# Three 128-token turns of a decoder trunk's token mixers, moved from TensorE to VectorE and DRAM

## The chip, the core and the metric

One core of a Trainium2 chip runs the whole program once. The metric is the device time of that run in microseconds (us), the median of several runs. A core has five engines with queues of their own: TensorE (PE in the profile; its weight loads are PEld), VectorE (DVE), ScalarE (ACT), GpSimd (POOL) and SyncE (SP). Each takes its instructions strictly in the order in which they were written into its queue, so an instruction that waits holds up everything behind it on that engine. Transfers (DMA) are issued here by SyncE, for the weights, and by GpSimd, for everything that bounces through DRAM.

## What is computed

A decoder trunk of two layers over 256 tokens of width 1024. In each layer, between two feed-forward halves, three token mixers work on the same normalised stream:

```python
h = layer_norm(ALPHA * x + 0.5 * swiglu(x, ...), ...)
(dn_q, dn_k, dn_v, dn_b, dn_a, dn_z, sw_q, sw_k, sw_v, xa_q, gates) = split(h @ w_in)
o_dn = deltanet_branch(...)            # gated delta rule, normalised rows times silu(z)
o_sw = sliding_window_attention(...)   # 128-key window, 8 heads, softmax with sinks
o_xa = memory_cross_attention(...)
merged = sum(sigmoid(gates) * einsum('bsnc,ncd->bsnd', [o_dn, o_sw, o_xa], w_branch))
h = layer_norm(ALPHA * h + merged @ w_out, ...)
return layer_norm(ALPHA * h + 0.5 * swiglu(h, ...), ...)
```

Two of these need a turn, a change of which axis lies on the 128 partitions: the softmax weights of the sliding mixer have queries on partitions and are wanted with keys there, and the output rows of the delta mixer have tokens on partitions and are wanted with channels there. The 256 tokens are two blocks of 128; "first" means the first block.

## The kernel before

All matrix products are made in split precision: an operand is a pair hi and lo, and each product is three matmuls, hi by hi, hi by lo and lo by hi (`mm3`, L139). Weights come as one stream of units of 128 x 1024 numbers, 512 KB each (`unit`, L104). For each unit SyncE issues the load into a `raw` tile (L115), ScalarE casts it to `whi` and VectorE subtracts to `wlo` (both in `split`, L125). There are four `raw` tiles and five of each of the others. A load is issued when a `raw` tile comes free, which is when VectorE has made the `wlo` of an older unit. `split` also makes the hi and lo parts of activations, so most of ScalarE's and VectorE's work has line L125.

Inside `mixers` the order of TensorE's instructions is pinned to the order of the code (`pe`, L129). The mixers come in the order cross attention (X), sliding window (S), delta (T). `gates(n)` (L1102) multiplies the stream by the gate weights in eight units and ends each half with two tanh; `branch(n, o)` (L1120) multiplies a mixer's output `o` by four units, in four quarters: first block left and right half, second block left and right half. `weave(work, steps)` (L145) runs the steps listed under n after the n-th unit or quarter of that work, and so fixes the places of the small matmuls. `tc.issue_after(i)` puts what follows behind i on i's engine; `held(f)` does so for all the instructions kept in `late`.

The steps that matter here, each once per layer:

- `w_scores(tb, hh)` (L832): scores and softmax weights of block tb for half hh of the heads; `w_turn(hh)` (L861) turns those of the first block by four PE transposes into PSUM (L137) and a ScalarE copy (L867); `w_leave` and `w_back` (L871, L882) turn those of the second block: VectorE transposes blocks of 32 x 32 (L875), four DMAs on GpSimd's queue write them to DRAM (L878), and DMAs read them back with the blocks in place (L888). `w_values(tb)` (L890) multiplies by the values.
- `leave_v` (L635) sends the delta mixer's values the same way (L640, L644, L648).
- `inverses` (L910) and `double` (L1030): GpSimd inverts 16 x 16 triangles by a chain of 30 small operations (L940, L941) on numbers that it reads back from DRAM (L928); TensorE doubles the inverses in seven steps, with small ScalarE and VectorE operations between them (the copy L995 after the third).
- `rec_o0` (L1094) makes the first block's delta output; `finish` (L1052) normalises it on VectorE and multiplies by silu(z) (L1060, L1061); `finish_turn(c)` (L1063) turns it by four PE transposes and splits it into `oT`, the operand of `branch(2)`.

The turns of block 0 are the steps `w_turn(0)`, `w_turn(1)` in `branch(0)` and `finish_turn(0)` in `gates(2)`.

Of the kernel before, what the change touches and what calls it, by code (L numbers as in the profile page):

```python
# [38 lines left out]
def tile_trunk(ctx, tc, x, xT, mem, memT_, wst, lnp, memln, cvw, rows, cst, out):  # L39
    nc = tc.nc  # L40
# [21 lines left out]
    def T(pool, shape, tag, dt=F32, bufs=None):  # L62
        pool = pn if pool is pu and tag in NEAR else pool
        kw = {} if bufs is None else {"bufs": bufs}
        return pool.tile(shape, dt, tag=tag, name=nm(tag), **kw)
# [4 lines left out]
    def at():  # L70
        return T(psT, [P, 512], "at")
# [64 lines left out]
    def transpose(*a):  # L136
        return pe(nc.tensor.transpose(*a))  # L137
# [422 lines left out]
    def mixers(l, hT, mkT, mv_, post0, post):  # L560
# [74 lines left out]
        def leave_v():  # L635
            turned_v = []
            for tb in range(2):
                z = T(p2, [P, 512], "t2", bufs=4)
                with tc.issue_after(wpr["end"]):
                    wpr["z"] = nc.vector.transpose(z, squares(vT, tb)).ins  # L640
                d = T(pd, [4, 32, 4, P], "tv")
                for a in range(4):
                    with tc.issue_after(late["inverses"]):
                        out_ = nc.gpsimd.dma_start(d[:, :, a].rearrange("t j x -> j t x"), z[32 * a:32 * a + 32].rearrange("j (t x) -> j t x", t=4)).ins  # L644
                turned_v.append(d)
            for tb in range(2):
                with tc.issue_after(out_):
                    late["pool"] = nc.gpsimd.dma_start(vin[:, tb].rearrange("p a h i -> p (a h i)"), turned_v[tb].rearrange("t j a x -> (t j) (a x)")).ins  # L648

        def land_v():  # L650
            for tb in range(2):
# [206 lines left out]
            wpr["end"] = nc.vector.reciprocal(sums, sums).ins  # L858
            late["act"] = [nc.scalar.mul(pr[:, h, :nk], pr[:, h, :nk], sums[:, h:h + 1]) for h in range(4)][-1].ins  # L859

        def w_turn(hh):  # L861
            if hh == 0:
                wpT[0] = T(p2, [P, 2, 4, P], "pt")
            ps = at().rearrange("p (h k) -> p h k", h=4)
            for h in range(4):
                transpose(ps[:, h, :], wpr[0, hh][:, h, :P], ident)
            nc.scalar.copy(wpT[0][:, :, 2 * hh:2 * hh + 2, :].rearrange("p v i q -> p i v q"), ps.rearrange("p (i v) q -> p i v q", v=2))  # L867

        left = []

# [19 lines left out]
        def w_values(tb):  # L890
            if not oS:
                oS.extend(T(pu, [P, 4, S], tag, F32R) for tag in ("u6", "u7"))
            ts = slice(tb * P, (tb + 1) * P)
            pso = at()
            for kb in range(tb + 1):
                for kv in range(2):
                    hs = slice(kv * 64, kv * 64 + 64)
                    if tb:
                        o, w = pso[hs].rearrange("p (y i x) -> p y i x", y=8, i=2), wpT[1][kb].rearrange("p h (a i v x) -> p (h a) i v x", a=4, i=2, v=2)[:, :, :, kv]
                    else:  # L900
                        o, w = pso[hs], wpT[0][:, kv].rearrange("p h q -> p (h q)")
                    matmul(o, swv[:, kb, hs], w, start=kb == 0, stop=kb == tb)
            if tb:
                for y in range(2):
                    late["act"], late["dve"] = split(*(t[:, 2 * y:2 * y + 2, ts].rearrange("p i (a x) -> p i a x", a=4) for t in oS), pso[:, y * S:y * S + S].rearrange("p (a i x) -> p i a x", a=4, i=2))
            else:
                late["act"], late["dve"] = split(oS[0][:, :, ts], oS[1][:, :, ts], pso.rearrange("p (h k) -> p h k", h=4))


        def inverses():  # L910

            cp = T(p2, [P, 16, 2, 4], "t2", bufs=4)
            for c in range(2):
                tmp = T(p2, [P, 4, P], "t2", bufs=4)
                nc.vector.tensor_tensor(tmp, AK[c][:, :, 0, :], over4(cs[:, C_NB:C_NB + P]), op=ALU.mult)
                nc.vector.tensor_reduce(cp[:, :, c], tmp.rearrange("p h (d i) -> p i h d", i=16), axis=AX.X, op=ALU.add)
            dr, dr2 = T(pd, [P, 16 * 8], "dr"), T(pd, [P, 8 * 8], "dr2")
            rows_ = cp.rearrange("p i c h -> p (i c h)")
            for d, r in ((dr, rows_), (dr2, rows_[:, 64:])):
                with tc.issue_after(late["pool"]):  # L920
                    late["pool"] = nc.gpsimd.dma_start(d, r).ins
            x_back()
            tm = [t.rearrange("p a h c -> p (a h c)") for t in TM]
            parts = [tm[0][:, 0:512], tm[0][:, 512:1024], tm[1][:, 0:512]]
            for t, (dst, d) in enumerate(zip(parts, (dr, dr, dr2))):
                src = d.rearrange("(d j) n -> d (j n)", j=16)[:, t % 2 * 512 + t // 2 * 512:][:, 0:512].unsqueeze(1).to_broadcast([8, 16, 512])
                with tc.issue_after(late["pool"]):
                    late["pool"] = nc.gpsimd.dma_start(dst, src).ins  # L928
            masks(1)

            y16 = T(p2, [P, 16, 8], "t2", bufs=4)
            pr16 = T(p2, [P, 15, 8], "t2", bufs=4)
            i16 = cs[:, C_I16:C_I16 + 16].unsqueeze(2).to_broadcast([P, 16, 8])
            with tc.issue_after(late["pool"]):
                nc.gpsimd.tensor_copy(y16, i16)
            for j in range(15):
                n = 15 - j
                row = (parts[j // 4][:, j % 4 * 128:j % 4 * 128 + 128] if j < 8 else parts[2][:, (j - 8) * 64:(j - 8) * 64 + 64]).rearrange("p (i n) -> p i n", n=8)
                row = row[:, j + 1 - j // 8 * 8:]
                nc.gpsimd.tensor_tensor(pr16[:, 0:n], row, y16[:, j:j + 1].to_broadcast([P, n, 8]), op=ALU.mult)  # L940
                nc.gpsimd.tensor_tensor(y16[:, j + 1:16], y16[:, j + 1:16], pr16[:, 0:n], op=ALU.add)  # L941
            late["inverses"] = nc.gpsimd.tensor_tensor(Y32.rearrange("p c h (d i) -> p (c h) d i", d=2), y16.rearrange("p i n -> p n i").unsqueeze(2).to_broadcast([P, 8, 2, 16]),
                                    cs[:, C_BD:C_BD + 32].rearrange("p (d i) -> p d i", d=2).unsqueeze(1).to_broadcast([P, 8, 2, 16]), op=ALU.mult).ins
# [108 lines left out]
        def finish(c, o, sq):  # L1052
            ms = T(p2, [P, 4], "oms")
            nc.scalar.activation(sq, o, AF.Square)
            nc.vector.tensor_reduce(ms, sq, axis=AX.X, op=ALU.add)
            nc.vector.scalar_tensor_tensor(ms, ms, 1.0 / P, qeps[:, c, :], op0=ALU.mult, op1=ALU.add)
            fr = T(p2, [P, 4], "ofr")
            rsqrt(fr, ms, T(p2, [P, 4], "oft"))
            on = fin[c] = T(p2, [P, 4, P], "t2", bufs=4)
            nc.vector.tensor_tensor(on, o, hb(fr), op=ALU.mult)  # L1060
            nc.vector.tensor_tensor(on, on, zs[:, c, :].rearrange("p (h e) -> p h e", h=4), op=ALU.mult)  # L1061

        def finish_turn(c):  # L1063
            if not oT:
                oT.extend(T(pu, [P, 4, S], tag, F32R) for tag in ("u8", "u9"))
            ps = sm().rearrange("p (h c) -> p h c", h=4)
            for h in range(4):
                transpose(ps[:, h, :], fin[c][:, h, :], ident)
            split(oT[0][:, :, c * P:(c + 1) * P], oT[1][:, :, c * P:(c + 1) * P], ps)
# [48 lines left out]
                yield  # L1118

        def branch(n, o):  # L1120
            us = [unit(behind=late["pairs"] if n == 1 and i > 1 else None) for i in range(4)]
            if not mg:
                mg.extend(T(pu, [P, D], f"u{4 + tb}") for tb in range(2))
            gt = gts[n]
# [21 lines left out]
            7: [lambda: w_scores(0, 0)],  # L1146
            8: [lambda: w_scores(0, 1)]})
        weave(branch(0, oX), {
            2: [lambda: w_turn(0)],
            3: [lambda: w_turn(1), leave_v, begin_inverse],  # L1150
            4: [lambda: w_scores(1, 0)]})
        weave(gates(1), {
            1: [double, lambda: w_values(0)],
            2: [lambda: w_scores(1, 1)],
            3: [double, lambda: held(lambda: w_leave(0))],
            5: [double, lambda: held(lambda: w_leave(1)), w_back],
            6: [double],
            7: [double, lambda: held(land_v)],
            8: [double, lambda: held(leave_q)]})
        weave(branch(1, oS), {  # L1160
# [2 lines left out]
            3: [rec_s1, lambda: held(land_q)],  # L1163
            4: [rec_r1]})
        weave(gates(2), {
            1: [rec_o0],
            2: [rec_qs, rec_v1],
            3: [rec_o1],
            5: [lambda: finish_turn(0)],
            8: [lambda: finish_turn(1)]})  # L1170

        def merge_turn(tb, q):
# [168 lines left out]
```

## Time and profile before

| | us |
|---|---|
| median of 3 runs (range) | 1261.83 (1261.32 to 1262.03) |
| the profiled execution, its own time | 1261.66 |
| its span, first to last instruction | 1259.9 |
| TensorE busy in the span | 1248.6 |
| VectorE, ScalarE, GpSimd busy | 880.0, 657.9, 257.0 |
| the mixers' weave, layer 1: `branch(0)` begins, `branch(2)` begins | 321.94, 410.80 |

The granted TensorE clock was 0.998. The span is 1.8 us shorter than the execution's time; what lies around it does not depend on the order inside. Times of rows are us from the span's start; the second layer runs the same code 623.4 us later (its first sliding turn stands at 950.87, that of layer 1 at 327.55). A timeline row gives start, duration, engine, line, operation, tiles written and read, shapes, and in brackets the idle time before it and what ended it. Rows of one line that follow each other may be merged; then x4 or the like stands behind, and one TensorE product in full float32 may stand as two.

### The profile page before, as it was taken

To read this page: it belongs to the slowest core of one execution; us is meant where nothing else is said; L and a number is where in the kernel's file an instruction comes from. 1 tells how busy PE (TensorE), PEld (TensorE's weight loads), DVE (VectorE), ACT (ScalarE), POOL (GpSimd) and SP (SyncE) were. 2 spreads that over 40 slices of the span, in tenths; PEclk is the share of its full clock that TensorE was granted. 3 is DMA by queue.
4 is the path that set the end of the run, shared out by engine and by line. 5 is a ranking of instruction groups with operands and counts; after the bars stand their busy time and mean duration, and the time that the engine had idled before them with its cause. 6 is when DMAs were issued, how large, how long until landed. Compare 5 with 4: busy or idle time off the path is not lost.

```text
span 1259.9 us, 18730 instructions
## 1 busy us (share of the span) xinstructions
PE 1248.6 (99%) x6836; PEld 1062.9 (84%) x6836; DVE 880.0 (70%) x1300; ACT 657.9 (52%) x978; POOL 257.0 (20%) x459
## 2 busy tenths in 40 slices
PE   9999999999999999999999999999999999999997
PEld 6888889999878888888888888899988788888886
DVE  5788567886768776665776665779777588666565
ACT  6556444655665544454454544356657654445441
POOL 1232102003541102221012220020055401122100
PEclk9999999999999999999999999999999999999999
DMA  8988767756565748887668886676565565588871
GB/s 288 318 276 272 262 217 215 225 182 181 182 185 156 247 140 254 245 239 223 219 206 240 261 259 206 214 236 211 161 192 173 163 213 205 187 247 242 243 228 73
DMA packets 82156, 273.60 MB, mean 217 GB/s; under 512 B 13424, under 2 KB 14864, under 8 KB 82064
## 3 DMA queue, kind: packets, MB, share of 16 engines
q1 hardware_dynamic: 66320, 232.40, 57.7%
q0 software_dynamic: 15600, 39.87, 11.0%
q8 instruction: 54, 0.88, 0.3%
q14 instruction: 38, 0.31, 0.1%
q10 hardware_dynamic: 144, 0.13, 0.0%
HBM read 252.20 MB, written 20.15 MB: 216 GB/s over the span
## 4 chain that ended last, share of the span: by engine, by line
PE 97%; ACT 1%; DMA 1%; DVE 0%; issue 0%; SPq 0%; DVEq 0%; ACTq 0%
PE acc L134 87%; PE at L134 4%; PE sm L134 3%; PE sm L137 1%; PE acc L332 1%; PE acc L333 1%; PE acc L335 1%; DMA raw<-in_wst_dram 1%; ACT pp L856 0%; PE at L137 0%; ACT pp L859 0%; ACT whi L125 0%; DVE h L291 0%; DVE h L296 0%; ACT w L995 0%
## 5 line engine op out<-in xcount | busy, mean ns | idle before, releaser
L125 DVE TENSOR_TENSOR wlo<-raw,whi 128x1024 fp32r<-128x1024 f32 (+2 forms) x405 | 485.7, 1208 | 254.6 <-ACT whi L125 252.5
L125 ACT CAST whi<-raw 128x1024 fp32r<-128x1024 f32 (+2 forms) x405 | 413.3, 1029 | 390.0 <-PE acc L134 293.2
L134 PE MATMUL acc<-whi,hT 128*128 128x512 f32 (+1 forms) x1824 | 562.6, 386 | 0.5 <-ACT whi L125 0.5
L134 PEld LDWEIGHTS acc<-whi,hT 128*128 128x128 f32 x1824 | 340.5, 188 | 69.8 <-ACT whi L125 2.2
L134 PE MATMUL acc<-wlo,hT 128*128 128x512 f32 (+1 forms) x912 | 350.9, 385 | 0.0
L134 PE MATMUL acc<-whi,u 128*128 128x512 f32 x812 | 260.3, 393 | 0.0
L134 PEld LDWEIGHTS acc<-wlo,hT 128*128 128x128 f32 x912 | 171.6, 188 | 32.9 <-DVE wlo L125 0.7
L134 PEld LDWEIGHTS acc<-whi,u 128*128 128x128 f32 x812 | 152.3, 188 | 33.7 <-issue 1.6
L362 POOL DMA_DIRECT2D tr<-t x176 | 95.9, 552 | 311.4 <-DVE t L356 309.3
L134 PE MATMUL acc<-wlo,u 128*128 128x512 f32 x406 | 158.3, 390 | 0.0
L134 PE MATMUL acc<-hT,whi 128*128 128x256 f32 x672 | 121.8, 284 | 0.0
L134 PEld LDWEIGHTS acc<-hT,whi 128*128 128x128 f32 x672 | 104.8, 192 | 0.0
L134 PE MATMUL acc<-hT,wlo 128*128 128x256 f32 x336 | 95.2, 283 | 0.0
L134 PEld LDWEIGHTS acc<-wlo,u 128*128 128x128 f32 x406 | 76.3, 188 | 15.3
L363 POOL DMA_DIRECT2D pt<-tr x44 | 24.6, 558 | 195.9 <-DMA tr<-t 134.0
L134 PEld LDWEIGHTS acc<-hT,wlo 128*128 128x128 f32 x336 | 64.4, 192 | 0.0
L353 ACT ACTIVATE t<-acc 128x256 f32<-128x256 f32 x88 | 33.4, 380 | 37.8 <-PE acc L134 37.7
L134 PE MATMUL acc<-u,u 128*128 128x512 f32 x186 | 46.4, 394 | 0.0
L354 DVE TENSOR_TENSOR t<-t,acc 128x256 f32<-128x256 f32 x88 | 36.7, 417 | 8.1 <-ACT t L353 4.1
L134 PEld LDWEIGHTS acc<-u,u 128*128 128x128 f32 x186 | 34.7, 188 | 7.5
L125 DVE TENSOR_TENSOR u<-pt,u 128x512 fp32r<-128x512 f32 x44 | 28.9, 657 | 14.1 <-ACT u L125 14.1
L1138 POOL TENSOR_TENSOR u<-u,gt 128x512 f32<-128x512 f32 x16 | 20.7, 1294 | 88.3 <-DVE gt L1135 88.3
(257 smaller groups left out, 1201.1 us busy)
## 6 DMA issues: line engine op xcount, KB each, us to landing
raw<-in_wst_dram SPq DMA_DIRECT2D x409, 512.0 KB, 4.5
tr<-t POOLq DMA_DIRECT2D x176, 64.0 KB, 4.0
pt<-tr POOLq DMA_DIRECT2D x44, 256.0 KB, 5.3
raw<-in_wst_dram SPq DMA_DIRECT2D x16, 324.0 KB, 5.1
gB<-in_lnp_dram SPq DMA_DIRECT2D x6, 512.0 KB, 5.5
bB<-in_lnp_dram SPq DMA_DIRECT2D x6, 512.0 KB, 6.3
tn<-pp POOLq DMA_DIRECT2D x16, 128.0 KB, 4.0
pt<-tn POOLq DMA_DIRECT2D x8, 256.0 KB, 6.0
```

Source lines behind the costliest of these rows:

```text
L125: return nc.scalar.copy(hi, src).ins, nc.vector.tensor_tensor(lo, src, hi.bitcast(F32), op=ALU.subtract).ins
L134: return pe(nc.tensor.matmul(*a, **k))
L137: return pe(nc.tensor.transpose(*a))
L332: nc.tensor.matmul(ps, hT[0][:, k, ts], hi[:, c], start=k == 0, stop=False)
L333: nc.tensor.matmul(ps, hT[0][:, k, ts], lo[:, c], start=False, stop=False)
L335: nc.tensor.matmul(ps, hT[1][:, k, ts], hi[:, c], start=False, stop=k == KD - 1)
L353: act = nc.scalar.activation(t[:, :, tb, :], g, AF.Silu).ins
L354: ins = nc.vector.tensor_tensor(t[:, :, tb, :], t[:, :, tb, :], u, op=ALU.mult).ins
L362: nc.gpsimd.dma_start(d[:, :, q].rearrange("b c x -> c b x"), z[32 * q:32 * q + 32].rearrange("c (b x) -> c b x", b=4))
L363: back = nc.gpsimd.dma_start(y, d.rearrange("b c q x -> (b c) (q x)")).ins
L1138: nc.gpsimd.tensor_tensor(mg[tb][:, js], mg[tb][:, js], gt[tb][:, js], op=ALU.add)
```

## The change

Three PE turns per layer go, and their work takes the path of `w_leave`:

- `w_turn` becomes `w_leave0` (a VectorE transpose of 128 x 512 per half), `w_out0` (four DMAs of 128 KB to DRAM, behind those of `leave_v`) and `w_back0` (two DMAs back, behind the reads of `leave_v`). `w_values(0)` reads the weights in the layout of the second block and moves from the first to the sixth unit of `gates(1)`. Its result is split in two pieces.
- `finish_turn(0)` becomes `finish_leave` behind `rec_o0` (a VectorE transpose of 128 x 512, four DMAs of 64 KB out, one of 256 KB back) and `finish_land` behind the seventh unit of `gates(2)`: the split from the tile that was read back, put behind the newest weight split on ScalarE and VectorE. The third and fourth weight units of `branch(2)` are split behind it (`behind=`). `finish_turn(1)` stays.
- `w_scores(1, 0)` comes before the last quarter of `branch(0)`, not behind it; `w_scores(1, 1)`, `w_leave(0)` and `w_leave(1)` with `w_back` come a unit sooner in `gates(1)`.
- In `inverses`, the second and third read of the numbers (`w<-dr`) are issued behind `masks(1)`, not ahead of it.

On TensorE, at the end of the second quarter of `branch(0)` in layer 1, this stood before (`acc` is a PSUM accumulator of the branch, `u_554` and `u_555` are hi and lo of X's output, `pp_3225` the sliding weights of half 0, `cs` holds the identity):

```order
L134 MATMUL acc_3339<-wlo_3319,u_554_3165 128x512
L134 MATMUL acc_3339<-whi_3318,u_555_3166 128x512
L137 MATMUL at_3354<-cs,pp_3225 128x128 x4
L134 MATMUL acc_3360<-whi_3300,u_554_3165 128x512
L134 MATMUL acc_3360<-wlo_3301,u_554_3165 128x512
```

and at the end of the third quarter this stands now, where the second turn stood (`swk` are the keys, `u_466` and `bB` hi and lo of the queries of block 1):

```order
L134 MATMUL acc_3355<-whi_3318,u_555_3166 128x512
L134 MATMUL at_3396<-swk_99,u_466_2584 128x512
L134 MATMUL at_3396<-swk_100,u_466_2584 128x512
L134 MATMUL at_3396<-swk_99,bB_2585 128x512
L134 MATMUL at_3401<-swk_99,u_466_2584 128x512
L134 MATMUL at_3401<-swk_100,u_466_2584 128x512
L134 MATMUL at_3401<-swk_99,bB_2585 128x512
L134 MATMUL acc_3424<-whi_3300,u_554_3165 128x512
```

The four transposes of each `w_turn` are gone from the queue, and the six products of `w_scores(1, 0)` stand one quarter earlier.

On ScalarE, around the end of `gates(2)` in layer 1, this stood before (`whi_4199`, `whi_4205` and `whi_4211` are units two, three and four of `branch(2)`; `u_731` is the hi part of `oT`; `sm_4122` and `sm_4185` are the turned first and second block in PSUM; `u_761` and `u_765` are units of the output projection; `gt<-acc` is a gate's tanh):

```order
L125 CAST whi_4199<-raw_4198 128x1024
L125 CAST u_731_4120<-sm_4122 128x4x128
L125 CAST whi_4205<-raw_4204 128x1024
L125 CAST whi_4211<-raw_4210 128x1024
L125 CAST u_761_4238<-raw_4237 128x1024
L1117 ACTIVATE gt_3954<-acc_4100 128x512
L125 CAST whi_4232<-raw_4231 128x1024
L125 CAST u_765_4259<-raw_4258 128x1024
L1117 ACTIVATE gt_3955<-acc_4101 128x512
L125 CAST u_731_4120<-sm_4185 128x4x128
```

and this stands now (`u_740` is the hi part of `oT`, `pt_4011` the tile read back from DRAM, `whi_4209` and `whi_4215` units three and four, `u_767` the output unit that was `u_765`):

```order
L125 CAST whi_4203<-raw_4202 128x1024
L125 CAST u_740_4165<-pt_4011 128x4x4x32
L125 CAST whi_4209<-raw_4208 128x1024
L125 CAST whi_4215<-raw_4214 128x1024
L125 CAST u_763_4242<-raw_4241 128x1024
L1143 ACTIVATE gt_3954<-acc_4109 128x512
L125 CAST whi_4236<-raw_4235 128x1024
L125 CAST u_767_4263<-raw_4262 128x1024
L1143 ACTIVATE gt_3955<-acc_4110 128x512
L125 CAST u_740_4165<-sm_4189 128x4x128
```

The queue is the same but for the second row, which waited for TensorE's turn and now waits for a DMA read.

On GpSimd, behind the reads of `leave_v` (`u_392<-tv`), the first block's weights go out (`tw_3384<-gt_3353`) and back (`pt_3391`), before the second block's (`tw_3546`, `tw_3630`, back into `pt_3635` and `pt_3636`):

```order
L878 DMA tw_3384<-gt_3353 32x8x128 x4
L651 DMA u_392_2081<-tv_3372 128x512
L651 DMA u_392_2081<-tv_3379 128x512
L885 DMA pt_3391<-tw_3384 128x512 x2
L896 DMA tw_3546<-u_626_3543 32x8x128 x4
L1026 COPY w_469_2587<-w_468_2586 32x4x32 x8
L896 DMA tw_3630<-bB_3627 32x8x128 x4
L906 DMA pt_3635<-tw_3546 128x512
L906 DMA pt_3636<-tw_3546 128x512
```

Six DMAs have come in between the delta values and the second block's weights.

The diff, cut to its core:

```diff
@@ leave_v
+            first["behind"] = out_
+            w_out0()
+            out_ = first["out"]
             for tb in range(2):
                 with tc.issue_after(out_):
                     late["pool"] = nc.gpsimd.dma_start(vin[:, tb]..., turned_v[tb]...).ins
+            w_back0()
...
-        def w_turn(hh):
-            if hh == 0:
-                wpT[0] = T(p2, [P, 2, 4, P], "pt")
-            ps = at().rearrange("p (h k) -> p h k", h=4)
-            for h in range(4):
-                transpose(ps[:, h, :], wpr[0, hh][:, h, :P], ident)
-            nc.scalar.copy(wpT[0][:, :, 2 * hh:2 * hh + 2, :]..., ps...)
+        def w_leave0(hh):
+            if not hh:
+                first["z"] = T(p2, [P, 1024], "gt")
+            nc.vector.transpose(first["z"][:, hh * 512:(hh + 1) * 512], wpr[0, hh][:, :, :P].rearrange("p h (m x) -> p m h x", m=4))
+
+        def w_out0():
+            first["d"] = T(pd, [8, 32, 4, P], "tw")
+            for a in range(4):
+                with tc.issue_after(first["behind"]):
+                    first["out"] = nc.gpsimd.dma_start(first["d"][:, :, a]..., first["z"][32 * a:32 * a + 32]...).ins
+
+        def w_back0():
+            wpT[0] = [T(p2, [P, 2, 512], "pt")]
+            for hh in range(2):
+                with tc.issue_after(late["pool"]):
+                    late["pool"] = nc.gpsimd.dma_start(wpT[0][0][:, hh], first["d"][4 * hh:4 * hh + 4]...).ins
...
@@ w_values
-            if tb:
-                for y in range(2):
-                    late["act"], late["dve"] = split(...)
-            else:
-                late["act"], late["dve"] = split(oS[0][:, :, ts], oS[1][:, :, ts], ...)
+            for y in range(2):
+                split(*(t[:, 2 * y:2 * y + 2, ts].rearrange("p i (a x) -> p i a x", a=4) for t in oS), pso[:, y * S:y * S + S]...)
...
@@ inverses
-            masks(1)
+                if not t:
+                    masks(1)
...
+        def finish_leave():
+            z = T(p2, [P, 4, P], "t2", bufs=4)
+            nc.vector.transpose(z, fin[0].rearrange("p h (m x) -> p m h x", m=4))
+            d = T(pd, [4, 32, 4, P], "tf")
+            for q in range(4):
+                nc.gpsimd.dma_start(d[:, :, q].rearrange("m r c -> r m c"), z[32 * q:32 * q + 32])
+            fin["back"] = T(p2, [P, 4, 4, 32], "pt")
+            nc.gpsimd.dma_start(fin["back"].rearrange("p q h x -> p (q h x)"), d.rearrange("m r q c -> (m r) (q c)"))
+
+        def finish_land():
+            oT.extend(T(pu, [P, 4, S], tag, F32R) for tag in ("u8", "u9"))
+            with tc.issue_after(newest[0]), tc.issue_after(newest[1]), tc.issue_after(fin["on"]):
+                fin["landed"] = split(*(t[:, :, 0:P].rearrange("p h (q x) -> p q h x", q=4) for t in oT), fin["back"])
...
         def branch(n, o):
-            us = [unit(behind=late["pairs"] if n == 1 and i > 1 else None) for i in range(4)]
+            us = [unit(behind={1: late.get("pairs"), 2: fin.get("landed")}.get(n) if i > 1 else None) for i in range(4)]
...
         weave(branch(0, oX), {
-            2: [lambda: w_turn(0)],
-            3: [lambda: w_turn(1), leave_v, begin_inverse],
-            4: [lambda: w_scores(1, 0)]})
+            2: [lambda: w_leave0(0)],
+            3: [lambda: w_leave0(1), leave_v, begin_inverse, lambda: w_scores(1, 0)]})
         weave(gates(1), {
-            1: [double, lambda: w_values(0)],
-            2: [lambda: w_scores(1, 1)],
-            3: [double, lambda: held(lambda: w_leave(0))],
-            5: [double, lambda: held(lambda: w_leave(1)), w_back],
-            6: [double],
+            1: [double, lambda: w_scores(1, 1)],
+            2: [lambda: held(lambda: w_leave(0))],
+            3: [double],
+            4: [lambda: held(lambda: w_leave(1)), w_back],
+            5: [double],
+            6: [double, lambda: w_values(0)],
...
         weave(gates(2), {
-            1: [rec_o0],
+            1: [rec_o0, finish_leave],
             2: [rec_qs, rec_v1],
             3: [rec_o1],
-            5: [lambda: finish_turn(0)],
+            7: [finish_land],
             8: [lambda: finish_turn(1)]})
```

More of the change, by code (lines that the diff above doesn't have):

```diff
@@ L859, in w_scores @@
             late["act"] = [nc.scalar.mul(pr[:, h, :nk], pr[:, h, :nk], sums[:, h:h + 1]) for h in range(4)][-1].ins
-        def w_turn(hh):
-            if hh == 0:
-                wpT[0] = T(p2, [P, 2, 4, P], "pt")
-            ps = at().rearrange("p (h k) -> p h k", h=4)
-            for h in range(4):
-                transpose(ps[:, h, :], wpr[0, hh][:, h, :P], ident)
-            nc.scalar.copy(wpT[0][:, :, 2 * hh:2 * hh + 2, :].rearrange("p v i q -> p i v q"), ps.rearrange("p (i v) q -> p i v q", v=2))
+        first = {}
+        def w_leave0(hh):
[6 more added lines that the diff above has]
+                with tc.issue_after(first["behind"]):
+                    first["out"] = nc.gpsimd.dma_start(first["d"][:, :, a].rearrange("m x c -> x m c"), first["z"][32 * a:32 * a + 32].rearrange("x (m c) -> x m c", m=8)).ins
+        def w_back0():
+            wpT[0] = [T(p2, [P, 2, 512], "pt")]
+            for hh in range(2):
+                with tc.issue_after(late["pool"]):
+                    late["pool"] = nc.gpsimd.dma_start(wpT[0][0][:, hh], first["d"][4 * hh:4 * hh + 4].rearrange("m x a c -> (m x) (a c)")).ins
         left = []
@@ L897, in w_values @@
                     hs = slice(kv * 64, kv * 64 + 64)
-                    if tb:
-                        o, w = pso[hs].rearrange("p (y i x) -> p y i x", y=8, i=2), wpT[1][kb].rearrange("p h (a i v x) -> p (h a) i v x", a=4, i=2, v=2)[:, :, :, kv]
-                    else:
-                        o, w = pso[hs], wpT[0][:, kv].rearrange("p h q -> p (h q)")
+                    o, w = pso[hs].rearrange("p (y i x) -> p y i x", y=8, i=2), wpT[tb][kb].rearrange("p h (a i v x) -> p (h a) i v x", a=4, i=2, v=2)[:, :, :, kv]
                     matmul(o, swv[:, kb, hs], w, start=kb == 0, stop=kb == tb)
-            if tb:
-                for y in range(2):
-                    late["act"], late["dve"] = split(*(t[:, 2 * y:2 * y + 2, ts].rearrange("p i (a x) -> p i a x", a=4) for t in oS), pso[:, y * S:y * S + S].rearrange("p (a i x) -> p i a x", a=4, i=2))
-            else:
-                late["act"], late["dve"] = split(oS[0][:, :, ts], oS[1][:, :, ts], pso.rearrange("p (h k) -> p h k", h=4))
+            for y in range(2):
+                split(*(t[:, 2 * y:2 * y + 2, ts].rearrange("p i (a x) -> p i a x", a=4) for t in oS), pso[:, y * S:y * S + S].rearrange("p (a i x) -> p i a x", a=4, i=2))
         def inverses():
@@ L1060, in finish @@
             nc.vector.tensor_tensor(on, o, hb(fr), op=ALU.mult)
-            nc.vector.tensor_tensor(on, on, zs[:, c, :].rearrange("p (h e) -> p h e", h=4), op=ALU.mult)
+            fin["on"] = nc.vector.tensor_tensor(on, on, zs[:, c, :].rearrange("p (h e) -> p h e", h=4), op=ALU.mult).ins
+        def finish_leave():
[10 more added lines that the diff above has]
+                fin["landed"] = split(*(t[:, :, 0:P].rearrange("p h (q x) -> p q h x", q=4) for t in oT), fin["back"])
         def finish_turn(c):
-            if not oT:
-                oT.extend(T(pu, [P, 4, S], tag, F32R) for tag in ("u8", "u9"))
             ps = sm().rearrange("p (h c) -> p h c", h=4)
```

## The prediction

> **What bounds the kernel now.** I read the page first: which engine is busy, and the chain that ended last.
>
> ```profile
> PE 1248.6 (99%) x6836; PEld 1062.9 (84%) x6836; DVE 880.0 (70%) x1300; ACT 657.9 (52%) x978; POOL 257.0 (20%) x459
> PE 97%; ACT 1%; DMA 1%; DVE 0%; issue 0%; SPq 0%; DVEq 0%; ACTq 0%
> ```
>
> TensorE is never out of work, and the end follows from it. So a microsecond of TensorE work that goes is a microsecond of the run, unless TensorE then waits for something. The waits of TensorE show how little there is of that now:
>
> ```profile
> PE sm L134 <- ACT w L995: 0.5, 2, 0.2
> ```
>
> In the mixers this is the only one: 0.2 us in each layer. So the question is not what VectorE, DRAM and GpSimd spend on the new path; it is whether TensorE, whose order is pinned, will arrive anywhere before its operand.
>
> **What goes from TensorE.** The chain in order of time has the three turns of layer 1 as pieces of their own, and those of layer 2 at the same size (its last is the fourth row):
>
> ```profile
> 327.55 0.44 PE at L137 x4
> ...
> 330.73 0.44 PE at L137 x4
> ...
> 401.98 0.44 PE sm L137 x4
> ...
> 1025.32 0.44 PE sm L137 x4
> ```
>
> Six turns by 0.44 us are 2.6 us. `w_values(0)` only moves; that its weights now lie in runs of 32 costs nothing, since the second block's product already reads them so and takes 1.87 us for twice the 1.01 us:
>
> ```profile
> 339.52 1.01 PE at L134 x4
> 373.77 1.87 PE at L134 x8
> ```
>
> **The wait in the doubling.** It comes about like this (timeline rows of ScalarE and TensorE):
>
> ```profile
> 350.71 0.60 ACT L1117 ACTIVATE gt<-acc 128x512 f32<-128x512 f32 x1 [0.32 <-PE acc L134]
> 351.49 0.30 ACT L1011 COPY w<-w 32x128 f32<-32x128 f32 x1 [0.18 <-DVE sk L852]
> 351.69 0.20 ACT L853 ACTIVATE sk<-sk 128x4 f32<-128x4 f32 x1
> ...
> 358.16 1.09 ACT L995 COPY w<-sm 32x128 f32<-32x128 f32 x4
> 358.75 1.14 PE L134 MATMUL sm<-w,w 32*32 32x32 f32 x32 [0.23 <-ACT w L995]
> ```
>
> From the tanh, which TensorE itself releases, ScalarE needs 7.45 us to the copies (350.71 to 358.16) and half of their 1.09 us for what TensorE reads first; TensorE comes 0.23 us sooner. In between ScalarE makes the softmax of the second scores' last half. With these scores a unit sooner, the sinks' exponential (L853) and the wait for VectorE around it stand before the tanh, and the rest stays behind it: ScalarE's stretch loses 0.2 and 0.18 us, TensorE's loses nothing. I take the wait as gone: 0.5 us in both layers, 3.1 us in all. If nothing of it goes, that is 0.5 us less.
>
> **Where the new path is covered.** The sliding weights: the second turn at 330.73 read them, so their VectorE transposes can end by 331.6. They are wanted behind the fourth doubling: 358.75 less two turns (0.9), the values themselves (1.0) and the wait (0.2) is 356.6, and the doubling takes 1.1: 357.7. The second block's path, by its rows below, takes 12 us from the transposes' end (359.00) to its last landing (366.7 and 4.4); with eight writes of `leave_v` at 0.55 us ahead the new one ends at about 348. The second block's own reads now need the tile that `w_values(0)` empties at 358.7, but wait for their last write longer than that, now as before: they go at 366.1 or, by the scores' earlier place, sooner, land by 371, and `w_values(1)` is at 373.77 less 1.1. VectorE's two transposes (1.3 us) and the first reading of the second scores (2.5 us) get ahead of these four weight splits:
>
> ```profile
> 332.97 4.63 DVE L125 TENSOR_TENSOR wlo<-raw,whi 128x1024 fp32r<-128x1024 f32 x4 [2.20 <-ACT whi L125]
> ```
>
> They fill its wait of 2.20 us and 1.6 us more, and TensorE wants the first of the four at about 340, behind the piece at 339.52 above. In the inverses the first read still goes first, GpSimd's work is the same, and the second read is wanted four steps of the chain later; TensorE reads the result only a quarter and a unit behind its end. All this I price at nothing; a cover 2 us too short would cost 2 us per layer.
>
> **The delta rows: the one place without cover.** The path of the first block's rows, from VectorE's rows of the last multiplications and of a transpose pair:
>
> ```profile
> 357.69 1.31 DVE L875 STREAM_TRANSPOSE bB<-pp 128x512 f32<-128x512 f32 x2 [0.39 <-ACT pp L859]
> ...
> 395.13 0.69 DVE L1060 TENSOR_TENSOR t<-t,ofr 128x512 f32<-128x512 f32 x1
> ...
> 402.79 0.69 DVE L1060 TENSOR_TENSOR t<-t,ofr 128x512 f32<-128x512 f32 x1
> 403.51 0.69 DVE L1061 TENSOR_TENSOR t<-t,u 128x512 f32<-128x512 f32 x1
> ```
>
> TensorE is 1.1 us ahead here (two turns, one wait), so L1060 starts at 394.0, L1061 0.72 behind it at 394.7, the transpose at 395.4, and it ends at 396.1. The DMAs, by GpSimd's rows (a write group of the mixers, and a group of the feed-forward with exactly these sizes and its read):
>
> ```profile
> 359.29 2.30 POOL L878 DMA_DIRECT2D tw<-bB  x4 [1.48 <-DVE bB L875]
> 366.14 1.06 POOL L888 DMA_DIRECT2D pt<-tw  x2 [2.57 <-DMA tw<-bB]
> ...
> 517.79 2.17 POOL L362 DMA_DIRECT2D tr<-t  x4 [3.97 <-DVE t L356]
> 524.12 0.56 POOL L363 DMA_DIRECT2D pt<-tr  x1 [4.16 <-DMA tr<-t]
> ```
>
> The first write goes 0.3 us after the transpose (359.00 to 359.29), at 396.4. From there to the read it takes 6.33 us in the feed-forward: the read goes at 402.7. Its landing, by what the trace says of a line's DMAs:
>
> ```profile
> L363 POOL DMA_DIRECT2D pt<-tr x44: 557/557/572, 30.7 to 1204.7; - x44
> DMA to landing us min/median/max: 2.9/5.3/6.2
> ```
>
> ```profile
> L888 POOL DMA_DIRECT2D pt<-tw x2: 536/537/538, 366.1 to 366.7; - x2
> DMA to landing us min/median/max: 4.3/4.3/4.4
> ```
>
> ```profile
> L644 POOL DMA_DIRECT2D tv<-t x8: 548/548/617, 330.2 to 334.1; - x8
> DMA to landing us min/median/max: 2.0/2.1/4.3
> ```
>
> The read takes between 2.9 and 6.2 us. It is nearest to the pair at 366, which shared the engines with one weight load, but is alone: I take 4.0 us. It lands at 406.7. (The writes: seven of eight in 2.0 to 2.3 us, the last, issued together with a weight load, in 4.3.)
>
> What this meets is ScalarE's queue, in which the split of the rows now stands ahead of branch 2's third unit:
>
> ```profile
> 402.97 0.58 ACT L125 CAST u<-sm 128x512 fp32r<-128x512 f32 x1
> 405.20 1.05 ACT L125 CAST whi<-raw 128x1024 fp32r<-128x1024 f32 x1 [1.65 <-PE acc L134]
> ...
> 411.66 1.05 ACT L125 CAST u<-raw 128x1024 fp32r<-128x1024 f32 x1
> ...
> 413.10 0.58 ACT L125 CAST u<-sm 128x512 fp32r<-128x512 f32 x1
> ```
>
> Before, that unit was cast at 405.20; now at 407.2, 0.5 us behind the landing. Branch 2 itself begins at 409.25 (410.80 less three turns and the wait), and the first rows are there. But the third unit's `raw` tile comes free only when VectorE has its `wlo`, 2.8 us behind the landing (0.5, 1.05 and 1.2), and into that tile goes the output unit cast at 411.66 in the rows above, which stands in ScalarE's queue ahead of the second block's split. So, counted from the landing: load issued at 2.85, landed at 6.6 (3.7 us, as that of a first load which others follow, below), cast from 6.6, tanh from 7.55, the second block's cast from 8.1 to 8.65; on VectorE the unit's `wlo` until 8.85 and the rows' lo part until 9.55, at 416.25.
>
> ```profile
> L115 SPq DMA_DIRECT2D raw<-in_wst_dram x1: 328/328/328, 384.1 to 384.1; - x1
> DMA to landing us min/median/max: 3.7/3.7/3.7
> ```
>
> TensorE wants that lo part for the third matmul of the second block:
>
> ```profile
> 410.80 0.47 PE L134 MATMUL acc<-whi,u 128*128 128x512 f32 x1
> ...
> 416.57 0.39 PE L134 MATMUL acc<-wlo,u 128*128 128x512 f32 x1
> 416.80 0.62 PE L134 MATMUL acc<-whi,u 128*128 128x512 f32 x2
> ```
>
> At 416.80 less 1.55, at 415.25. TensorE waits 1.0 us, in each layer: 2.0 us. Every microsecond by which the read lands later costs one, down to a landing at 405.7, ahead of which nothing waits. With the bounds: a last write of 2.1 us instead of some 4 and a read of 2.9 give 403.7 and no wait; the mixers' own 6.85 us from write to read (359.29 to 366.14) and 6.2 us give 409.4 and 3.7 us per layer.
>
> **The sum.** 2.6 + 0.5 - 2.0 = 1.1 us: 1261.66 becomes 1260.6 for the profiled execution. That execution lies 0.2 us below the median of the runs shown (1261.83), so I put the new median at 1260.7.
>
> **The rivals.**
>
> *The rows land in time.* The windows speak for it, in their last column of GB/s: traffic is a third less where the rows travel than in the feed-forward.
>
> ```profile
> 395.00:411.00 16.00, 16.00 (x80) 13.43 (x79) 13.64 (x27) 9.21 (x12) 0.00 (x0) 1.00 0.56 164
> 500.00:560.00 60.00, 60.00 (x267) 49.68 (x266) 37.30 (x45) 30.09 (x40) 14.21 (x26) 1.00 0.82 242
> ```
>
> Against it: VectorE's next `wlo`, two operations behind the transpose, frees a weight load at about 398, just when the last write goes, and the following load goes ahead of the read. If the last write lands in 2.1 us and the read in 2.9, the whole 3.1 us stay: 1258.7. The Trainium skill, "DMA: Bandwidth & Descriptors", section "Anatomy of one DMA — SWDGE (gpsimd) path", gives such a DMA 2.0 us and its bytes at 436 GB/s, by which the write would take 2.15 us and the read 2.6 us, and this rival would be the forecast. The trace agrees for seven of the eight writes above, and not for the eighth or the reads.
>
> *The rows land late, and ScalarE's queue holds the weights back.* The same mechanism with the mixers' 6.85 us and a read of 5.3, the feed-forward's median: landing at 408.5, a wait of 2.8 us per layer, 5.7 us against 3.1: 1264.4. It decides from a landing at 407.25, where wait and gain are equal; beyond 408.5 the loss exceeds 0.2%, about what a measurement of this kernel can tell from no change. The Trainium skill, "VectorE: DVE Perf Modes", section "Rules for kernel authors", advises TensorE for a 128 x 128 transpose where PSUM may receive it; it prices the operation alone, not an engine that is full.
>
> *The doubling's wait grows instead.* VectorE now has the transposes of `w_leave(0)` to make between the parts of that softmax. If they hold ScalarE up, so that the copies come 0.5 us late instead of 0.2, the forecast's gain of 0.5 us becomes a loss as large: 1261.7, within 0.2%.
>
> That the turns stay on TensorE can't be: they are not in its queue.
>
> **How the numbers follow.** Forecast, a wait between 0.3 and 2.8 us per layer: 0.52. In time: 0.31. Late: 0.13. Doubling: 0.04. Faster by over 0.2% (below 1259.3) is the second, 0.31; slower by over 0.2% the third, 0.13; the rest 0.56. The range takes in the gain in full with 0.2 us for the runs' spread, 1258.5, and reaches up to most of the late case, 1263.8.
>
> **What would show it.** In the new profile: L137 sixteen times instead of 32 on `pp` and eight instead of sixteen on `t`; PE waits on L995 gone; the rows' read (L1084) landing 10 to 11 us after the transpose (L1079); ScalarE idle before the split of `pt` for some 4 to 5 us, ended by that DMA; and TensorE waiting for L125 on `u` or `whi` in branch 2, about 1 us per layer. I am wrong if TensorE waits nowhere there, if it waits at `w_values`, or if the landing is late and it still doesn't wait.

## The result and the profile after

| | before | changed |
|---|---|---|
| median, us (range) | 1261.65 (1260.60 to 1262.34, 8 runs) | 1258.07 (1257.59 to 1259.17, 8 runs) |
| profiled execution, own time (span) | 1261.66 (1259.9) | 1257.86 (1256.1) |
| TensorE busy | 1248.6 | 1245.3 |

The ratio is 0.9976, 95% interval 0.9966 to 0.9985: 3.6 us faster, 2.6 us below the forecast and 0.4 us below the range. Repeated, the changed kernel took 1258.30 us against 1261.45, ratio 0.9977 (0.9968 to 0.9985).

The page after, the lines of busy time and of the chain:

```profile
PE 1245.3 (99%) x6812; PEld 1059.7 (84%) x6812; DVE 884.2 (70%) x1308; ACT 654.9 (52%) x976; POOL 271.3 (22%) x481
PE 96%; DVE 2%; DMA 1%; ACT 1%; issue 0%; POOL 0%; DVEq 0%; ACTq 0%; POOLq 0%
```

TensorE has lost 24 instructions and 3.3 us. VectorE's share of the chain has grown from 0 to 2%. TensorE's waits name what is new there:

```profile
PE acc L134 <- ACT u L125: 0.2, 1, 0.2
PE acc L134 <- DVE u L125: 0.2, 1, 0.2
```

The waits on the doubling's copy (now L1008) are gone, and two on the split of `u` have come, in the third branch. The line L137, which makes all PE transposes, shows that the turns left (before: 32 on `pp` and 16 on `t`):

```profile
L137 PE MATMUL at<-cs,pp x16: 270/272/273, 304.1 to 927.1; 128*128 128x128 f32 x16
L137 PE MATMUL sm<-cs,t x8: 270/272/273, 407.4 to 1030.0; 128*128 128x128 f32 x8
```

**The doubling.** TensorE's rows there, after:

```profile
355.13 0.39 PE L134 MATMUL acc<-whi,hT 128*128 128x512 f32 x1
355.45 0.89 PE L134 MATMUL sm<-w,w 32*32 32x32 f32 x32
356.27 1.08 PE L134 MATMUL at<-pt,swv 128*64 128x512 f32 x4
```

and before:

```profile
358.13 0.39 PE L134 MATMUL acc<-whi,hT 128*128 128x512 f32 x1
358.75 1.14 PE L134 MATMUL sm<-w,w 32*32 32x32 f32 x32 [0.23 <-ACT w L995]
359.82 0.50 PE L134 MATMUL acc<-whi,hT 128*128 128x512 f32 x1
```

Read them from start to start. The 32 small products began 0.62 us after the product ahead of them and now begin after 0.32; they lasted 1.07 us until the next and now 0.82. What went is 0.55 us per layer, of which the bracket showed 0.23: the copies let the 32 products go in two lots, and the second lot's wait lies inside the merged row. (Before, products 1 to 16 started from 358.75 to 359.15 and the other 16 from 359.30 on, behind the fourth copy, which ended at 359.25.) Layer 2 lost the same 0.55 us.

**The third branch.** The chain in order of time, layer 1, from the rows' transpose on (the pieces of 0.02 to 0.52 us between these are left out):

```profile
394.05 0.72 DVE t L1079
...
395.06 1.33 POOL tf L1082 x3
...
396.69 3.77 DMA tf<-t
...
401.09 3.96 DMA pt<-tf
...
405.64 1.06 ACT whi L125
...
406.72 1.24 DVE wlo L125
...
407.97 3.67 DMA raw<-in_wst_dram
...
411.67 1.06 ACT u L125
...
412.75 1.01 DVE u L125
...
413.89 0.70 DVE u L125
...
414.63 2.56 PE acc L134 x10
```

It is the path that the prediction described, link by link: rows out, rows back, third unit's cast and `wlo`, the load into its tile, the output unit's cast, on VectorE that unit's lo part and the second block's, TensorE. And TensorE at its end:

```profile
413.11 0.39 PE L134 MATMUL acc<-whi,u 128*128 128x512 f32 x1
413.74 0.50 PE L134 MATMUL acc<-whi,u 128*128 128x512 f32 x1 [0.24 <-ACT u L125]
414.07 0.40 PE L134 MATMUL acc<-wlo,u 128*128 128x512 f32 x1
414.63 0.73 PE L134 MATMUL acc<-whi,u 128*128 128x512 f32 x2 [0.16 <-DVE u L125]
```

Again the brackets show half. The four starts are 0.63, 0.33 and 0.56 us apart; without waits three such products take 0.23 each. From the branch's start (407.79) to the product at 414.63 are 6.84 us; where nothing waits (410.80 to 416.80 in the kernel before, and an experiment below) it is 6.00. So the wait is 0.84 us in layer 1 and, read the same way, 0.28 us in layer 2.

**Ahead of the change.** The profiled executions differ by 3.8 us, but 0.98 us of that stands before any changed instruction. The same piece of the chain, before and after:

```profile
184.65 2.82 PE at L134 x24
```

```profile
183.67 2.82 PE at L134 x24
```

It comes from the first 10 us, where TensorE waits for the first weights. In the thirteen profiles of this study this code is the same, and TensorE's 61st product into `acc` starts anywhere from 19.98 to 21.26 us (before 21.11, after 20.13). One more stall of about 0.4 us, for which the profile names no cause ("issue"), comes and goes behind the mixers of layer 1:

```profile
451.74 1.33 PE L137 MATMUL sm<-cs,h 128*128 128x128 f32 x8 [0.37 <-issue]
```

It is in the profiles of before and after, not in that of the changed kernel's repetition. So a single profile is compared below from that 61st product to the last: before 1225.81 us, changed 1223.04 and, repeated, 1223.15, that is 2.8 and 2.7 us less.

### The profile page after: what moved, and what is told of

It is laid out like the page before. It is cut to its first block, busy times and chain, and to the rows that moved or that the text cites. A ratio compares the mean times of both kernels' runs of the same rounds, so it can differ in the third digit from the quotient of the medians.

```text
span 1256.1 us, 18718 instructions
## 1 busy us (share of the span) xinstructions
PE 1245.3 (99%) x6812; PEld 1059.7 (84%) x6812; DVE 884.2 (70%) x1308; ACT 654.9 (52%) x976; POOL 271.3 (22%) x481
## 4 chain that ended last, share of the span: by engine, by line
PE 96%; DVE 2%; DMA 1%; ACT 1%; issue 0%; POOL 0%; DVEq 0%; ACTq 0%; POOLq 0%
PE acc L134 85%; PE at L134 4%; PE sm L134 3%; PE acc L332 1%; PE sm L137 1%; PE acc L333 1%; PE acc L335 1%; DMA raw<-in_wst_dram 1%; DVE wlo L125 1%; ACT whi L125 0%; DMA pt<-tf 0%; PE sm L1243 0%; DMA tf<-t 0%; DVE u L125 0%; ACT u L125 0%
## 5 line engine op out<-in xcount | busy, mean ns | idle before, releaser
L125 ACT CAST u<-pt 128x512 fp32r<-128x512 f32 x46 | 28.2, 614 | 24.1 <-DMA pt<-tr 15.4
```

The source lines that it names most:

```text
L125: return nc.scalar.copy(hi, src).ins, nc.vector.tensor_tensor(lo, src, hi.bitcast(F32), op=ALU.subtract).ins
```

## The experiments

The theory after the first profile: the sliding part gives 1.6 us per layer (two turns, and a doubling wait larger than its bracket), and the delta part gives 0.44 and loses 0.3 to 0.9 again in the third branch. The rival: the rows land in time, as in the prediction's second case, whose 1258.7 is near the result. Medians of before are 1261.45, 1261.42 and 1261.38 us in the three groups of runs.

**The changed kernel again** (group 1).

> The changed kernel unaltered, for the spread of its executions. Theory: its first profile began TensorE's steady stream (the matmul that stood at 9.78 us before and at 8.84 us after) 0.94 us sooner than the kernel before, in code that the change doesn't touch; this is an accident of the first loads, so a second profile can show any start between 8.8 and 9.8 us, and the gain from there to the end stays 2.8 us. Rival: the start belongs to the changed program, and is 8.8 us again. The median should be 1258.1, 3.6 us under the kernel before, by both.

1258.30 us. Its steady stream began 0.33 us later than in the first profile, not at the same time, so the start does not belong to the changed program alone. The rest was 2.7 us, where 2.8 were expected.

**Each part alone** (group 1). Delta rows turned by TensorE again:

```diff
-            1: [rec_o0, finish_leave],
+            1: [rec_o0],
-            7: [finish_land],
+            5: [lambda: finish_turn(0)],
```

> The changed kernel with the delta rows turned by TensorE again, at the old place. Theory: the delta part loses more than it gains, because the branch behind waits in each layer (0.8 and 0.4 us by TensorE's rows) for what stands in ScalarE's queue behind the rows that are read back, against 0.44 us for the turn: without it the time is 0.3 us less than the changed kernel's, 1257.8, and TensorE has no wait in the third branch. Rival (the rows land in time): the turn's 0.9 us come back in full, 1259.0.

1257.99 us, ratio 0.9972 (0.9961 to 0.9983), and no wait in the third branch. The interval alone would allow the rival's 1259.0, but all six runs were below it (the slowest 1258.91). And the delta part alone, the same lines the other way round in the kernel before:

> The kernel before with the delta part alone. Theory: two turns go, 0.9 us, and the waits of 0.8 and 0.4 us come: 0.3 us slower than before, 1262.0, with TensorE's rows in the third branch held up in both layers. Rival (the rows land in time): 0.9 us faster, 1260.8. Rival (the forecast's size, 1.0 us of wait per layer): 1.1 us slower, 1262.8.

1262.37 us, ratio 1.0007 (0.9998 to 1.0015): 0.9 us slower by the medians, and 0.96 us by the profile from the 61st product on. The rival of rows that land in time asked for 0.9 us faster, and the interval excludes that. It does not tell the theory's 1262.0 from the 1262.8 of the other rival, and the trace lies between them: waits of 0.30 and 1.23 us, 1.5 in all, where the theory put 1.2 and the rival 2.0. In its layer 2 the rows landed at 1031.20 and TensorE got the second block's lo part 9.52 us later; its waits in the mixers:

```profile
PE acc L134 <- ACT u L125: 0.6, 1, 0.6
PE sm L134 <- ACT w L995: 0.5, 2, 0.2
...
PE acc L134 <- DVE u L125: 0.2, 1, 0.2
```

So the whole gain is the sliding part's, and turning the delta rows off TensorE as written costs what it saves or more.

**Take the wait away, from two sides** (group 2). The third unit ahead of the rows (cut; the line that makes the tile `oT` moves along, into `finish_turn`):

```diff
-            us = [unit(behind=...) for i in range(4)]
+            us = []
+            for i in range(4):
+                if (n, i) == (2, 3):
+                    with tc.high_priority(offset=AHEAD):
+                        finish_land()
+                us.append(unit(behind=...))
...
-            7: [finish_land],
```

> The changed kernel with one exchange in ScalarE's and VectorE's queues: the third weight unit of the third branch is split ahead of the rows that come back from DRAM, only the fourth behind them. Theory: the wait in the third branch comes from that unit standing in the queue behind the rows, since its raw tile frees late and the load into it holds up the second block's split; with the unit ahead, its cast starts at about 402.5 instead of 405.6 us in layer 1, and the waits of 0.8 and 0.4 to 0.7 us are gone: 1.2 to 1.6 us less than the changed kernel's 1258.2, 1256.8. Rival (TensorE waits for the rows themselves): no change, 1258.2. Rival (the rows' split is now late, because it stands behind a cast that waits for a weight tile): slower, above 1259.

1256.88 us, ratio 0.9960 (0.9946 to 0.9974), the theory's number. ScalarE's rows, after and then here:

```profile
405.12 0.62 ACT L125 CAST u<-pt 128x512 fp32r<-128x512 f32 x1 [4.59 <-DMA pt<-tf]
405.64 1.99 ACT L125 CAST whi<-raw 128x1024 fp32r<-128x1024 f32 x2
...
411.67 1.05 ACT L125 CAST u<-raw 128x1024 fp32r<-128x1024 f32 x1 [1.66 <-DMA raw<-in_wst_dram]
412.62 0.59 ACT L1143 ACTIVATE gt<-acc 128x512 f32<-128x512 f32 x1
413.11 0.57 ACT L125 CAST u<-sm 128x512 fp32r<-128x512 f32 x1
```

```profile
402.42 1.05 ACT L125 CAST whi<-raw 128x1024 fp32r<-128x1024 f32 x1 [1.67 <-PE acc L134]
405.89 0.62 ACT L125 CAST u<-pt 128x512 fp32r<-128x512 f32 x1 [2.42 <-DMA pt<-tf]
...
410.31 1.05 ACT L125 CAST u<-raw 128x1024 fp32r<-128x1024 f32 x1
411.26 0.59 ACT L1143 ACTIVATE gt<-acc 128x512 f32<-128x512 f32 x1
411.75 0.58 ACT L125 CAST u<-sm 128x512 fp32r<-128x512 f32 x1
```

The rows landed nearer to the branch than in the changed kernel (2.2 us ahead of its start instead of 2.7), and TensorE waited nowhere in it (6.00 us in both layers); its list of waits has one row, at the program's first product:

```profile
PE sm L1247 <- DVE pp L1244: 1.5, 1, 1.5
```

It was the queue, not the rows.

The other side, rows that leave one step sooner:

```diff
-            4: [rec_r1]})
+            4: [rec_r1, rec_o0, finish_leave]})
...
-            1: [rec_o0, finish_leave],
+            1: [],
```

> The changed kernel with the first block's delta output, its normalisation and its way out one step sooner, in the last quarter of the second branch instead of behind the first unit of the last gates. Theory: the rows land 2 to 2.7 us sooner, at about 402.7 us in layer 1, which is ahead of the point from which they hold up ScalarE's queue; the waits of the third branch go, 1.2 to 1.6 us: 1256.8. Rival (the wait does not come from the landing): no change, 1258.2. A rival with the other sign: the product for this output then follows the product of the step before it and waits for one of the two small PSUM tiles, some 0.5 us per layer, which takes most of the gain.

1257.02 us, ratio 0.9962 (0.9949 to 0.9975). The rows landed only 1.1 us sooner in layer 1 (403.96), which was enough: 3.65 us ahead of the branch. The interval just reaches the rival's 1258.2; the trace decides: the 6.00 us of the branch took 6.01 and 6.11, and TensorE waited for no PSUM tile. Both cures together:

> Both cures together: the rows leave one step sooner, and the third unit is split ahead of them. Theory: each cure alone took the whole wait, so together they give no more: 1256.9. Rival (each took a part of it, and some is left in either): 0.3 us or more below 1256.9.

1256.47 us, ratio 0.9959 (0.9947 to 0.9972). By the medians that is 0.4 us below one cure, which is what the rival asked for. By the profiles, from the 61st product on, it is 1221.30 us against 1221.43 and 1221.54, and neither cure alone left more than 0.11 us of wait in the branch: no more to be had there, as the theory says. With five runs of each and intervals that nearly coincide, the 0.4 us may be chance; this was not settled. And the cure in the delta part alone:

> The kernel before with the delta part alone, and the third weight unit of the third branch split ahead of the rows. Theory: the delta part alone lost 0.9 us because its waits (1.56 us in the two layers of its profile) exceeded the two turns (0.9 us); without the waits the turns show in full: 0.9 us less than before, 1260.5. Rival (moving these rows through DRAM costs something else too, such as VectorE's or the DMA engines' time): no gain, 1261.4.

1260.17 us, ratio 0.9989 (0.9981 to 0.9998): with the queue mended the two turns show (1.2 us by the medians, 0.9 by the profile).

**Let the rows land later** (group 2).

```diff
-            nc.gpsimd.dma_start(fin["back"]..., d...)
+            for n in range(2):
+                nc.gpsimd.dma_start(fin["back"]..., d...)
```

> The changed kernel with the rows read back twice, the second read behind the landing of the first; nothing else is different. Theory (every microsecond by which the rows land later costs one in each layer, once they land too late): the second read adds its issue and its landing, 3 to 4.5 us per layer, and all of that is lost: 6 to 9 us more than the changed kernel's 1258.2, about 1266. Rival (TensorE's operand has some slack left, as in the case where the rows land in time): less than half of the delay shows, below 1262.

1263.09 us, ratio 1.0013 (1.0003 to 1.0022): 4.9 us more than the changed kernel, a miss. The rows landed 4 us later in layer 1 (410.18 against 405.05, with a stream that began 1.13 us later), but ScalarE's queue came out in another order too: the output unit's cast stands behind the second block's split, so that the load was no longer in the way. What is left is TensorE waiting for the rows themselves at the branch's start, then 1.1 us in each layer inside the branch, for the rows' lo part and the weight units split behind it, and 0.5 us at 428.28, behind the branch. ScalarE and TensorE:

```profile
410.24 0.62 ACT L125 CAST u<-pt 128x512 fp32r<-128x512 f32 x1 [8.59 <-DMA pt<-tf]
...
415.52 0.58 ACT L125 CAST u<-sm 128x512 fp32r<-128x512 f32 x1
416.87 1.05 ACT L125 CAST u<-raw 128x1024 fp32r<-128x1024 f32 x1 [0.77 <-DMA raw<-in_wst_dram]
```

```profile
410.91 0.50 PE L134 MATMUL acc<-whi,u 128*128 128x512 f32 x1 [1.75 <-ACT u L125]
...
414.26 0.50 PE L134 MATMUL acc<-wlo,u 128*128 128x512 f32 x1 [0.17 <-DVE wlo L125]
```

It tells nothing of the slope along the first path. The layers that kept the order do, below.

**The wait in the doubling** (group 1 and 2). Only the second scores sooner, in the kernel before (with `w_leave(0)` and `w_leave(1)` a unit sooner, as in the change):

```diff
-            3: [lambda: w_turn(1), leave_v, begin_inverse],
-            4: [lambda: w_scores(1, 0)]})
+            3: [lambda: w_turn(1), leave_v, begin_inverse, lambda: w_scores(1, 0)]})
...
-            1: [double, lambda: w_values(0)],
-            2: [lambda: w_scores(1, 1)],
+            1: [double, lambda: w_values(0), lambda: w_scores(1, 1)],
```

> The kernel before with only the second sliding scores, and the two ways out of their weights, a unit sooner; all three turns stay on TensorE. Theory: the wait in the doubling goes, and it is larger than the 0.23 us of idle time that the row showed, since the 32 small products behind it are stretched as well (1.07 us against 0.82): 0.55 us per layer, 1.1 us in all, 1260.6. Rival (the forecast's size): 0.5 us, 1261.2. Rival: the wait went because the two copies of the turns left ScalarE, not because of the scores: no change, and the wait on the copies stays.

1265.03 us, ratio 1.0032 (1.0020 to 1.0044): none of the three. The wait on the copies is gone from the list, and from start to start 0.55 us went in each layer; but another wait came:

```profile
PE at L134 <- DVE pp L844: 4.3, 2, 2.7
```

VectorE's rows say why:

```profile
342.08 1.23 DVE L125 TENSOR_TENSOR wlo<-raw,whi 128x1024 fp32r<-128x1024 f32 x1 [2.68 <-ACT whi L125]
343.23 0.68 DVE L844 SCALAR_TENSOR_TENSOR pp<-at,cs 128x512 f32<-128x512 f32 x1
```

There are two PSUM tiles of this kind. `w_values(0)` holds one until its split, whose VectorE part stands at 346.35; the first score product holds the other until L844, which stands in VectorE's queue behind a `wlo` that waits for ScalarE. The second score product, and all of TensorE, waits for that. So, in this kernel, the scores can come sooner because `w_values(0)` has moved away. The cleaner test, the sliding part alone with the scores at their old places:

```diff
-            3: [lambda: w_leave0(1), leave_v, begin_inverse, lambda: w_scores(1, 0)]})
+            3: [lambda: w_leave0(1), leave_v, begin_inverse],
+            4: [lambda: w_scores(1, 0)]})
...
-            1: [double, lambda: w_scores(1, 1)],
+            1: [double],
+            2: [lambda: w_scores(1, 1)],
```

(with `w_leave(0)` and `w_leave(1)` back in units 3 and 5)

> The kernel with the sliding part alone (1258.0), with the second scores and the ways out of their weights put back to their old places; the two sliding turns stay off TensorE. Theory: the wait in the doubling returns with its true size, 0.55 us per layer: 1.1 us more, 1259.1, and TensorE waits for the copies behind the third doubling step again, 0.2 us in the idle column. Rival (the wait went with the turns, whose copies left ScalarE): no change, 1258.0. Rival (scores that come later also need a PSUM tile while VectorE is late): more than 2 us, above 1260.

1259.38 us, ratio 0.9981 (0.9972 to 0.9990): 1.4 us more than with the scores moved, where 1.1 were expected. The interval excludes neither rival; the trace does: TensorE waits for no PSUM tile here, the wait is back, and the 32 products take 1.07 us again:

```profile
355.86 1.14 PE L134 MATMUL sm<-w,w 32*32 32x32 f32 x32 [0.22 <-ACT w L1008]
356.93 1.08 PE L134 MATMUL at<-pt,swv 128*64 128x512 f32 x4
```

**The reads and the masks** (group 3): `masks(1)` behind all three reads again.

> The changed kernel with the second and third read of the numbers for the 16 x 16 inverses issued ahead of the masks again, as before the change. Theory: GpSimd's chain behind them is off the path that sets the end, so nothing changes: 1258.2, and TensorE waits for nothing new. Rival (the earlier masks gave part of the gain that the rows of the profile leave unexplained, 0.4 to 0.8 us): 1258.6 to 1259.0.

1258.53 us, ratio 0.9975 (0.9965 to 0.9985): 0.2 to 0.5 us above the changed kernel's two medians, inside the ranges of its runs, and nearer to the rival's 1258.6 than to the theory's 1258.2. From the 61st product on it is 0.3 to 0.4 us longer, and its layer 2 waits 0.96 us in the third branch where the others waited 0.28 and 0.72. No effect is shown; one of up to 0.4 us is not excluded.

## Why the prediction was right in its mechanism and wrong in its sum

- **TensorE bounds, and six turns are 2.6 us: right.** 24 products went, and the delta part alone, with its queue mended, shows two of the turns at 0.9 to 1.2 us.
- **"I take the wait as gone: 0.5 us in both layers": mis-sized, the first error.** It went, through the scores, but it was 1.1 us. The prediction read the bracket of one row; the stretch inside the row was as large.
- **Sliding weights, VectorE's splits, reads and masks at nothing: right, to the 0.4 us that the masks leave open.** With the sliding part alone TensorE waits nowhere in the mixers. Some 0.15 us per layer came beyond turns and wait, and the runs place most of it. From the first product of `branch(0)` to the 16 small products of the fifth doubling step TensorE took 40.84 us before (321.94 to 362.78), 39.87 with the turns gone and the scores at their old places, and 39.28 with the scores moved too (layer 2: 40.86, 39.87 and 39.28). So two turns, with the values' move, are worth 0.97 to 0.99 us per layer where 0.88 were priced, and the earlier scores 0.59 where the wait alone is 0.55.
- **"TensorE waits 1.0 us, in each layer: 2.0 us": right mechanism, mis-sized, the second error.** Its rule was: no wait to a landing at 405.7 with the branch at 409.25, and one for one from there, so wait = landing - start + 3.55. In the eight layers with that queue order:

| kernel, layer | landing | branch starts | wait by the rule | wait measured |
|---|---|---|---|---|
| changed, 1 | 405.05 | 407.79 | 0.81 | 0.84 |
| changed, 2 | 1026.81 | 1030.01 | 0.35 | 0.28 |
| again, 1 | 405.48 | 408.13 | 0.90 | 0.86 |
| again, 2 | 1027.06 | 1030.01 | 0.60 | 0.72 |
| masks back, 1 | 405.75 | 408.47 | 0.83 | 0.74 |
| masks back, 2 | 1027.90 | 1030.40 | 1.05 | 0.96 |
| delta alone, 1 | 406.71 | 410.08 | 0.18 | 0.30 |
| delta alone, 2 | 1031.20 | 1033.49 | 1.25 | 1.23 |

  The rule holds to 0.12 us. (Rows that leave one step sooner keep this order too: 3.65 and 3.71 us ahead of the branch the rule has no wait, and 0.01 and 0.11 us were measured.) So the size that failed is that of the path to the landing: forecast 2.55 us ahead of the branch, measured 2.3 to 3.4, 2.8 in the mean. The landing came 11.0 us after the transpose in layer 1, and ScalarE sat idle for 4.59 us before the rows' split, both as foretold. The mean wait is 0.74 us; the two layers of the first profile cost 1.1 us instead of 2.0.
- **The rival "in time" came nearest to the time (1258.7) and is still not what happened.** With rows in time TensorE would not have waited for them, and the delta part alone would be faster, not slower. That the time agrees is luck: of the 2.6 us between forecast and median 0.9 are the smaller wait in the branch, 0.6 the larger wait in the doubling, 0.3 the turns and scores beyond their price, and 0.8 lie outside the part of the profile compared here.
- **The price of the read.** The trace's two rows for reads in the mixers gave 4.3 and the forecast took 4.0; this read took 3.4 and 4.0, and 2.9 to 4.6 in the other kernels of this study. The Trainium skill's formula ("DMA: Bandwidth & Descriptors", "Anatomy of one DMA — SWDGE (gpsimd) path") would have made it, as an estimate, 2.6; none of the 20 reads of these rows came to that, and the measurement decides.

The sum, from the 61st product on: 2.6 for the turns, 1.1 for the doubling, less 1.1 for the branch, is 2.6, and with the 0.3 beyond their price 2.9 against 2.8 measured. The median's 3.6 has 0.8 more, 0.4 in the repetition. Starts alone differ by up to 1.3 us between profiles, so that a part of the medians' difference may be chance; this was not settled.

## What to carry to other kernels

A wait of a bound engine is read from start to start over the whole group of instructions, against the same group where it does not wait; the idle time in brackets can be less than half of it. When work is moved off a full engine through a slow path, look not only at when it lands but at what stands behind it in an in-order queue: here one weight unit ahead of the rows instead of behind them was worth 1.3 us, and gave the best kernel with a single cure (1256.88 us, 1256.47 with both). And a time that agrees with a case is no proof of that case: do each part alone.

## What the runs showed that was not expected

- Four writes of 64 KB issued 0.54 us apart by GpSimd do not land alike: 2.0, 2.1, 3.0 and 3.8 us after their issue in layer 1, and nearly the same in layer 2 and in every other run (the last 3.8 to 4.0). The weight load at 396.50 was issued 0.2 us ahead of the last one and 0.36 us behind the third. In all 18 layers it and the last write take the same time to within 0.1 us (3.75 and 3.77 here), so the load may be what slows the last two; no run has these writes without it. The median hides this:

```profile
L1082 POOL DMA_DIRECT2D tf<-t x8: 551/551/551, 395.1 to 1018.9; - x8
DMA to landing us min/median/max: 2.0/2.5/3.8
```

- In code that is the same in all thirteen profiles, TensorE's 61st product started up to 1.3 us apart (the changed kernel's two profiles 0.33), which is half of the 2.8 us that the change gives behind it.
